# A hybrid decoder trunk on one core: heads cut into steps of one engine each and issued by a running count of the engines' time

## The chip, the cores and the metric

The kernel runs on one core of one Trainium2 chip. The core has TensorE (PE, with its weight loads shown apart as PEld), VectorE (DVE), ScalarE (ACT), GpSimd (POOL) and SyncE (SP, which here only issues DMAs). The metric is the device time of one execution in microseconds, from the hardware; lower is better. The time before is the median of three executions.

## What is computed

Two layers. Each projects x (512 x 2048) with one combined weight matrix, runs three groups of heads (128 columns each), gates every head, projects back, and normalises:

```python
h = x @ w_in                                    # split into fq fk fv fg f_logit  dq dk dv dg  iq ik iw  mq mg
# A) 6 forgetting heads: causal softmax(q k' * scale + c_query - c_key) v, c = cumsum(log_sigmoid(f_logit + b))
# B) 6 sparse heads: rotary q and k; an indexer of 16 small heads picks 128 keys per query; softmax over these
# C) 4 heads into 256 memory tokens: k and v from mem @ w_mem_kv
y = concat(fox, dsa, mem) * silu(gates)
y = y @ w_out
x = layer_norm(alpha * x + y, gain, bias)
```

All of it is float32 accuracy. Every matrix product is made of three matmuls on rounded operands: with a = ah + al and b = bh + bl, it is ah bh + ah bl + al bh. `hi` is made by ACT (a copy that rounds), `lo` by DVE (a subtraction); this pair is called a split.

## The kernel before

**Stages and chunks.** The weights are cut into blocks of 128 x 2048, called chunks, in the order in which TensorE uses them (`stream`). A layer has: the memory's values and keys (`mv`, `mk`), a small block with the indexer's keys and the forget logits (`small`), eight blocks of indexer queries (`iq`), the products for everything that is read by rows (`vs`: the queries and keys of the first four heads of each group, all values, all gates, the memory heads' queries and gates), eight blocks for the queries and keys of the last two heads of each group (`fq 4`, `fk 4`, `fq 5`, `fk 5`, `dq 4`, `dk 4`, `dq 5`, `dk 5`: the head chunks), and the output's products (`out`).

**Fast products.** The `vs` and `out` products use a scheme with seven block products in place of eight (`PRODUCTS`, line 72). Their weight blocks are sums and differences of the stored ones: T1, T3, T2 = T1 + a block, T4 = T2 + a block. Before the change they come about in four ways (`product`, lines 127 to 140): as they are stored (`wall`); summed in DRAM by DMAs on GpSimd's queue and then loaded (`sum`, made by `weight_sums`, line 423); `pair`, two blocks fetched and added on DVE (`pair_w`, line 278: values' T1 for pairs 1 to 5); or `grown`, where a DMA on GpSimd's queue adds a block onto weights that are in SBUF already (`grow_w`, line 286, and `make_w`): in the output, T2 for product Q6 is grown out of P7's T3, and T4 for Q4 out of Q6's. The values run twice over six pairs of columns: a first pass of ten chunks per pair (P1, P7, P2, Q6, Q4), then a second of four (Q5, Q3).

**Loads and splits.** While TensorE works on half-chunk n, the loop (from line 1203) issues the load of a chunk two further on (SP), the growth or pair addition of a later half, and the split of half n + 3 (`split_w`). Seven buffers hold raw weights, four hold splits; 69 slots of 128 x 512 hold everything else, and PSUM has eight banks.

**What sets the order of the heads.** Each engine runs its own queue in order. Work beside the chunks is written as Python generators that are put on a list by `begin` and moved on by `tick`, one step per call. `tick` is called at the middle and at the end of a chunk, and in the head chunks also a quarter of the way in and after three quarters. `TURNS` (line 52) fixes by hand at which half-chunk a head starts (`head_turn`, line 1026). A head (`attend`, line 748) has these steps:

1. scores into three PSUM banks (L224 to L226 through `product`), then on DVE the bias and the row's maximum (L767), on ACT the exponential with its sum (L771). The normalisation (L775 on DVE, L778 on ACT) is put off to the list `before`, which is emptied at a few places in the loop.
2. load of the gates (SP, L999), a turn later load of the values.
3. transposes of the probabilities (L792), their split.
4. transposes of the gates, tanh on ACT and a product on DVE (`gate`, line 507), split of the values (vh on ACT, vl on DVE, L804).
5. the product with the values (L810), and on DVE the gated result (L523).

A step that has operations on several engines issues them all at once, so a PE instruction of the step stands in PE's queue behind what it needs from ACT and DVE in the same step or the step before. Queries and keys of the first four heads of a group are loaded, transposed and split by `qk_head` (line 1013), those of the last two come out of the head chunks (lines 1333 to 1341). `rope` (line 591) does its last addition on GpSimd for loaded heads, on DVE for heads out of chunks. A forgetting head's bias is made on GpSimd (`forget_bias`, line 673). `all_sums` (line 462) issues the DRAM sums a few ticks apart: the values' in the index stage and the values, the output's T3 and T1 in the head stage and the output.

**The output.** Its products read the heads' results as left operands. P1 and P7 need the first eight heads, Q6 and later products all sixteen. `early_operands` and `first_difference` make the first operands during the last head chunks, `late_operands` the rest.

Of the kernel before, what the change touches and what calls it, by code (L numbers as in the profile page):

```python
# [33 lines left out]
SCALE = HD ** -0.5  # L34

# [16 lines left out]
TURNS = {1: ("f", 1), 2: ("d", 0), 3: ("f", 4), 5: ("d", 1), 6: ("f", 2), 7: ("f", 5), 9: ("d", 2),  # L52
         10: ("f", 3), 11: ("d", 4), 13: ("d", 3), 15: ("d", 5)}
MEM_TURNS = {3: 3}
# [39 lines left out]
PAIRED = {"T1": ((0, 0), (0, 1))}  # L94
# [26 lines left out]
def stream():  # L121
# [53 lines left out]

@with_exitstack
def kernel(
# [13 lines left out]
    nc = tc.nc  # L191
# [3 lines left out]
    slots = ctx.enter_context(tc.tile_pool(name="slots", bufs=69))  # L195
# [10 lines left out]

    def slot(name, dt=F32, w=512):
        return slots.tile([P, w], dt, tag="s", name=uid(name))
# [7 lines left out]
    def split(src, hi, lo):  # L216
        nc.scalar.activation(hi, src, AF.Copy)  # L217
        nc.vector.tensor_tensor(lo, src, hi.bitcast(F32), op=ALU.subtract)  # L218
# [30 lines left out]
    def load_w(i, pieces=2, some=(0, 1)):  # L249
        if i < len(chunks) and chunks[i][4][0] != "grown":  # L250
# [3 lines left out]
            if chunks[i][0] == "out" and chunks[i][2][0] == "P7":  # L254
# [86 lines left out]

    held = {i for pair in lends.values() for i in pair}
# [35 lines left out]
    make_identity(nc, ident)  # L378
# [65 lines left out]
    def paced(gen, steps=3):  # L444

        n = 0
        for _ in gen:
            n += 1
            while now[1] == "kv":
                yield 1  # L450
            yield {"heads": 2, "out": 3, "index": 1 + n % 2}.get(now[1], steps)

    def value_sums(l):

        for p in range(PAIRS + 1):
            for n, pair in ((0, p), (1, p - 1)):
                if 0 <= pair < PAIRS:
                    yield from weight_sums("val", l, ("T3",), (pair,), (n,))
        for n in range(2):
            yield from weight_sums("val", l, ("T1",), range(IN_DRAM), (n,))  # L460

    def all_sums():


        for l in range(DEPTH):
            yield from paced(value_sums(l))
            while now != (l, "heads"):
                yield 1
            yield from paced(weight_sums("out", l, ("T3", "T1"), range(2)))
# [10 lines left out]
    before = []  # L480
# [18 lines left out]
    def run_all():  # L499
        while active:  # L500
            tick()

    gates, qs, ks = {}, {}, {}
    ys, left = {}, {}
    masks, chosen, making = {}, set(), []

    def gate(key, ps):

        t = slot("tanh")
        nc.scalar.activation(t, ps, AF.Tanh, scale=0.5)  # L510
        nc.vector.scalar_tensor_tensor(t, t, 1.0, ps, op0=ALU.add, op1=ALU.mult)
        gates[key] = t

    def heads_out(n, key, po):
# [4 lines left out]
        for t in range(2):  # L519
            if e == 0:  # L520
# [3 lines left out]
                                           g[:, c], op0=ALU.mult, op1=ALU.mult)  # L524

# [10 lines left out]
    def mem_head(l, j):  # L536
        load_head(("mq", j), MEMQ, j)
        km = slot("kmem", F32R)
        nc.sync.dma_start(km.bitcast(F32), km_d[l][j])
        yield 3  # L540
        tp = turned(("mq", j), "qk")
        q = slot("qh", F32R), slot("ql", F32R)
        split(tp, *q)
        yield 1
        k2 = (km[:, 0:256], km[:, 256:512])
        ps = [bank("sm"), bank("sm")]
        for qb in range(4):
            product(ps[qb // 2][:, (qb % 2) * 256:(qb % 2 + 1) * 256],
                    tuple(a[:, qb * P:(qb + 1) * P] for a in q), k2, True, True)
        nm, sums, rec = small("nm", 4), small("sums", 4), small("rec", 4)  # L550
        pr = [slot("pm"), slot("pm")]
# [3 lines left out]
        nc.vector.tensor_scalar(nm, nm, SCALE, None, op0=ALU.mult)  # L555
        for qb in range(4):
            cols = slice((qb % 2) * 256, (qb % 2 + 1) * 256)
            nc.scalar.activation(pr[qb // 2][:, cols], ps[qb // 2][:, cols], AF.Exp,
                                 bias=nm[:, qb:qb + 1], scale=SCALE, accum_out=sums[:, qb:qb + 1])
        del km, k2, q  # L560
        vm = slot("vmem", F32R)
        nc.sync.dma_start(vm.bitcast(F32), vm_d[l][j])
        load_head(("mg", j), MEMQ + 1, j)
        yield 1
        nc.vector.reciprocal(rec, sums)
        yield 1
# [939 lines left out]
```

## Time and profile before

| | |
|---|---|
| time, median of 3 runs | 1951.5 us (1949.57 to 1953.13) |
| the profiled execution: time, span | 1955.5 us, 1953.7 us |
| mean granted TensorE clock | 0.993 |
| ACT busy, POOL busy | 1056.9 us (54%), 450.3 us (23%) |
| DMA | 495 MB in 190900 packets, mean 253 GB/s |

The span is from the first to the last instruction of one execution; the time of that execution is 1.8 us more. Busy times of the engines overlap. A row of the table of stretches gives the busy time of each engine in one stretch of the span; a row of the groups gives a line of the kernel, the engine, what is written from what, the shape, how often, its busy time, the mean length of one in nanoseconds, and the idle time of the engine ahead of it with what ended most of it. A matmul's length there includes its way through the array, so matmuls overlap; the distance from one start to the next is what one costs.

### The profile page before, as it was taken

Reading aid. Unit: us, or ns where it says so; the run is one execution under the profiler, and the core shown is the slowest. Engines: PE = TensorE matmul, PEld = TensorE weight load, DVE = VectorE, ACT = ScalarE, POOL = GpSimd, SP = SyncE. Lnnn points to the kernel's source line nnn. Section 1 sums busy time; section 2 is a strip of 40 time slices with the busy share of each in tenths; the row PEclk is TensorE's granted clock in tenths of the full one; section 3 lists DMA queues with packets and bytes.
Section 4 is the critical chain, followed back from the end, with each engine's and each line's share of the span. In section 5 each row is a group of like instructions: output and inputs, shape, how many; then the busy total and the mean of one; then the engine's idle time right before and its main releaser. Section 6 shows DMA issues by size and latency. Waiting matters only on the chain.

```text
span 1953.7 us, 26942 instructions
## 1 busy us (share of the span) xinstructions
PE 1897.2 (97%) x9218; PEld 1604.7 (82%) x9218; DVE 1525.5 (78%) x2455; ACT 1056.9 (54%) x1690; POOL 450.3 (23%) x659
## 2 busy tenths in 40 slices
PE   9999999999999999999999999999999999899997
PEld 8998888888888877787889988888888788777886
DVE  6889778888666667778887897889886666677898
ACT  5776444445455665555476764444454556655553
POOL 0122112211112222271041231211111122222611
PEclk9999999999999999999999999999999999999999
DMA  9888889989999676999878899887799996759975
GB/s 351 297 238 216 248 256 266 279 243 275 324 304 288 210 189 173 283 221 303 283 228 278 243 239 276 264 252 222 210 272 324 310 284 210 189 173 292 260 223 140
DMA packets 190900, 495.17 MB, mean 253 GB/s; under 512 B 18656, under 2 KB 71904, under 8 KB 184172
## 3 DMA queue, kind: packets, MB, share of 16 engines
q1 hardware_dynamic: 144204, 295.24, 44.3%
q0 software_dynamic: 46560, 198.23, 41.6%
q8 instruction: 72, 1.18, 0.2%
q14 instruction: 64, 0.52, 0.1%
HBM read 439.89 MB, written 147.87 MB: 301 GB/s over the span
## 4 chain that ended last, share of the span: by engine, by line
PE 74%; DVE 10%; ACT 6%; DMA 5%; issue 4%; POOL 1%; SPq 0%; DVEq 0%; ACTq 0%; POOLq 0%
PE v L224 16%; PE v L226 16%; PE v L225 16%; PE c L226 4%; PE c L224 4%; PE c L225 4%; PE z L225 3%; PE z L226 3%; PE z L224 3%; DVE wlo L218 2%; DMA raw<-in_wall_dram 2%; DVE rope L595 1%; ACT bt L771 1%; ACT whi L217 1%; DVE pthl L218 1%
## 5 line engine op out<-in xcount | busy, mean ns | idle before, releaser
L218 DVE TENSOR_TENSOR wlo<-raw,whi 128x1024 fp32r<-128x1024 f32 (+1 forms) x497 | 605.2, 1223 | 245.1 <-ACT whi L217 243.1
L217 ACT ACTIVATE whi<-raw 128x1024 fp32r<-128x1024 f32 (+1 forms) x497 | 523.3, 1056 | 458.8 <-PE v L226 308.5
L224 PE MATMUL v<-whi,vxh 128*128 128x512 f32 x768 | 300.3, 391 | 3.2 <-ACT vraw L980 3.2
L226 PE MATMUL v<-whi,vxl 128*128 128x512 f32 x768 | 299.1, 389 | 0.0
L225 PE MATMUL v<-wlo,vxh 128*128 128x512 f32 x768 | 298.9, 389 | 0.0
L224 PE MATMUL v<-whi,xh 128*128 128x512 f32 x576 | 224.2, 389 | 0.0
L226 PE MATMUL v<-whi,xl 128*128 128x512 f32 x576 | 224.1, 389 | 0.0
L225 PE MATMUL v<-wlo,xh 128*128 128x512 f32 x576 | 224.1, 389 | 0.0
L224 PE MATMUL c<-xh,whi 128*128 128x512 f32 (+1 forms) x544 | 202.3, 372 | 0.1
L226 PE MATMUL c<-xh,wlo 128*128 128x512 f32 (+1 forms) x544 | 199.3, 366 | 0.0
L225 PE MATMUL c<-xl,whi 128*128 128x512 f32 (+1 forms) x544 | 198.5, 365 | 0.0
L225 PE MATMUL z<-wlo,yh 128*128 128x512 f32 (+1 forms) x434 | 169.1, 390 | 5.9 <-DVE wlo L218 5.9
L224 PEld LDWEIGHTS v<-whi,vxh 128*128 128x128 f32 x768 | 144.2, 188 | 33.5 <-ACT vraw L980 4.0
L226 PEld LDWEIGHTS v<-whi,vxl 128*128 128x128 f32 x768 | 144.1, 188 | 30.4
L224 PE MATMUL z<-whi,yh 128*128 128x512 f32 (+1 forms) x434 | 168.6, 389 | 0.0
L225 PEld LDWEIGHTS v<-wlo,vxh 128*128 128x128 f32 x768 | 144.2, 188 | 29.4
L226 PE MATMUL z<-whi,yl 128*128 128x512 f32 (+1 forms) x434 | 167.9, 387 | 0.0
L226 PEld LDWEIGHTS v<-whi,xl 128*128 128x128 f32 x576 | 108.1, 188 | 22.6
L224 PEld LDWEIGHTS v<-whi,xh 128*128 128x128 f32 x576 | 108.1, 188 | 22.6
L225 PEld LDWEIGHTS v<-wlo,xh 128*128 128x128 f32 x576 | 108.1, 188 | 22.4
L992 POOL DMA_DIRECT2D v<-vraw x96 | 52.5, 548 | 273.9 <-DVE vraw L969 148.6
L226 PEld LDWEIGHTS c<-xh,wlo 128*128 128x128 f32 x544 | 102.4, 188 | 12.1
(224 smaller groups left out, 3494.4 us busy)
## 6 DMA issues: line engine op xcount, KB each, us to landing
raw<-in_wall_dram SPq DMA_DIRECT2D x330, 512.0 KB, 7.2
sum<-in_wall_dram POOLq DMA_DIRECT2D x44, 1024.0 KB, 11.0
raw<-sum SPq DMA_DIRECT2D x72, 512.0 KB, 8.1
v<-vraw POOLq DMA_DIRECT2D x144, 256.0 KB, 6.7
raw<-in_wall_dram POOLq DMA_DIRECT2D x56, 512.0 KB, 8.0
vraw<-v SPq DMA_DIRECT2D x96, 256.0 KB, 5.2
other<-in_wall_dram SPq DMA_DIRECT2D x80, 256.0 KB, 9.1
grown<-in_wall_dram POOLq DMA_DIRECT2D x64, 256.0 KB, 9.8
```

The source lines that it names most:

```text
L217: nc.scalar.activation(hi, src, AF.Copy)
L218: nc.vector.tensor_tensor(lo, src, hi.bitcast(F32), op=ALU.subtract)
L224: nc.tensor.matmul(ps, ah, bh, start=start, stop=False, skip_group_check=more)
L225: nc.tensor.matmul(ps, ah, bl, start=False, stop=False, skip_group_check=more)
L226: nc.tensor.matmul(ps, al, bh, start=False, stop=stop, skip_group_check=more)
L595: nc.vector.tensor_tensor(t2[a:a + n], ps[b:b + n], sin[b:b + n], op=ALU.mult)
L771: nc.scalar.activation(pr[b][:, off:off + w], pr[b][:, off:off + w], AF.Exp, bias=nm[:, qb:qb + 1], scale=-1.0, accum_out=sums[:, qb:qb + 1])
L992: nc.gpsimd.dma_start(to, t)
```

## The change

Heads are no longer moved on by `tick` at fixed turns. Their generators yield ahead of each piece of work the engine that does it, how many PSUM banks it takes, a time ahead of which it must not be issued, and a condition. `Clock` keeps a running count of each engine's time while the program is written out, with a price by engine, operation and size. `advance`, called after every product of three matmuls in the head, values and output chunks, issues those pieces whose inputs are done by the count, whose banks are free and whose engine is not far ahead of PE. At most three heads are in work at once (`ACTIVE`), and a head waits until enough slots are free (`enough`). Ahead of an output product, `drain` issues head pieces until that product's operands have been issued.

Other edits: the normalisation of the probabilities goes from ACT to DVE; the low half of the values' split and the last addition of every rotary head go to GpSimd; the loads of gates and values come at a head's start. The weight splits of the head chunks are pieces with a due time as well. In the values, T3 for pairs 1 to 5 is fetched as two blocks and added by GpSimd, not summed in DRAM. In the output, T2 is summed in DRAM and loaded, and P7's weights aren't kept. `all_sums` issues at another pace and goes on to the output's sums directly. The first operands of the output are made when the first eight heads are done, the differences when the output begins. The residual's stores come one tick after its scaling. The diff, cut to its core:

```diff
+SOON, LATER, URGENT, DUE = 0.7, 4.0, 5.0, 14.0
+SLOTS = 69
+PACE = 8
+R_ATTEND, R_QK, R_LOAD, R_MEM = 4, 5, 4, 8
+START = (("f", 0), ("f", 1), ("d", 0), ("f", 4), ("d", 1), ("f", 2), ("m", 3), ("f", 5), ("d", 2),
+         ("f", 3), ("d", 4), ("d", 3), ("d", 5))
+ACTIVE = 3
-PAIRED = {"T1": ((0, 0), (0, 1))}
+PAIRED = {"T1": ((0, 0), (0, 1)), "T3": ((0, 1), (1, 1))}
-            if name in GROWN:
+            if name in GROWN and (kind == "val" or name == "Q4"):
...
+class Clock:
+    def charge(self, eng, op, args, kw):
+        if eng == "PE":
+            n = args[0].shape[-1]
+            if op == "transpose":
+                took = 0.109 if n == P else 0.06
+            else:
+                took = max(n / 2400 + 0.0134, 0.058)
+            self.at["PE"] += took
+            return
...
+                took = 0.00105 * n + (0.17 if op == "tensor_tensor_reduce" else 0.07)
...
+                took = 0.003 * n + 0.2 if op == "tensor_tensor" else 0.0008 * n + 0.27
+        self.at[eng] = max(self.at[eng], self.at["PE"], self.floor) + took
...
+    def enough(n):
+        return now[1] == "out" or live() + n <= SLOTS - 2 * KT - 3
...
-                nc.vector.tensor_tensor(d, d, others.pop((i, 2 * h + e)), op=ALU.add)
+                eng = nc.gpsimd if chunks[i][2][0] == "P7" else nc.vector
+                eng.tensor_tensor(d, d, others.pop((i, 2 * h + e)), op=ALU.add)
...
+            yield from paced(weight_sums("out", l, ("T3", "T1", "T2"), range(2)))
+            while l + 1 < DEPTH and now[0] == l:
                 yield 1
-            yield from paced(weight_sums("out", l, ("T3", "T1"), range(2)))
...
+    def fits(f, room):
+        eng, t = f[2], clock.at["PE"]
+        if f[4] is not None and not f[4]():
+            return False
+        if eng == "PE":
+            return f[0] <= t and f[3] <= room
+        return f[0] <= max(t, clock.at[eng]) and clock.at[eng] <= t + (SOON if now[1] == "heads" else LATER)
+    def advance():
+        while flows:
+            t = clock.at["PE"]
+            freed[:] = [x for x in freed if x > t]
+            room = 8 - banks["main"] - banks["held"] - len(freed)
+            some = [f for f in flows if fits(f, room)]
+            if not some:
+                return
+            step_flow(min(some, key=lambda f: f[5] if f[6] > t + URGENT else -1.0))
+    def drain(done):
+        start = clock.at["PE"]
+        while not done():
+            advance()
+            if not done():
+                clock.at["PE"] += 0.2
...
+        def scores(b, blocks):
+            yield "PE", 1
+            ps = bank("s")
...
+            yield "DVE",
...
+            yield "ACT",
...
+        yield "DVE", 0, 0.0, after(scored, 3)
+        nc.vector.reciprocal(rec, sums)
...
+            nc.vector.tensor_scalar(pr[b][:, c], pr[b][:, c], rec[:, qb:qb + 1], None, op0=ALU.mult)
...
+        def values_of():
+            yield "ACT", 0, v_there
...
+            split_hi(t, v[0])
+            yield "POOL",
+            nc.gpsimd.tensor_tensor(v[1], t, v[0].bitcast(F32), op=ALU.subtract)
...
+        yield "PE", 1, 0.0, after(turns, 5)
...
+            drain(lambda: (PRODUCTS[name][1], 2 * col + 1) in left)
...
+            if (kind, j) in HEAD_CHUNKS:
+                splits[n + 3] = flow(split_steps(n + 3), 1e9, clock.at["PE"] + DUE)
+            else:
+                split_w(n + 3)
```

More of the change, by code (lines that the diff above doesn't have):

```diff
@@ L340, in split_w, with split_steps @@
                 raw[i][h] = None
+    def split_steps(n):
+        i, h = divmod(n, 2)
+        if i < len(chunks):
+            r = raw[i][h]
+            hi = whl.tile([P, H], F32R, tag="whi", name=uid("whi"))
+            lo = whl.tile([P, H], F32R, tag="wlo", name=uid("wlo"))
+            qs = [(r, slice(0, H))]
+            if isinstance(r, list):
+                qs = [(r[c], slice(c * 512, (c + 1) * 512)) for c in range(2)]
+            yield "ACT",
+            for t, q in qs:
+                split_hi(t, hi[:, q])
+            yield "DVE",
+            for t, q in qs:
+                split_lo(t, hi[:, q], lo[:, q])
+            parts[n] = (hi, lo)
+            if i not in grows and i not in held:
+                raw[i][h] = None
+    splits = {}
     held = {i for pair in lends.values() for i in pair}
@@ L442, in weight_sums, with paced @@
                         yield
[L444 removed]
+    def paced(gen, steps=PACE):
         n = 0
@@ L448, in paced @@
             n += 1
-            while now[1] == "kv":
+            while now[1] in ("kv", "second"):
                 yield 1
-            yield {"heads": 2, "out": 3, "index": 1 + n % 2}.get(now[1], steps)
+            yield {"heads": 1, "out": 3, "index": 1 + n % 2}.get(now[1], steps)
     def value_sums(l):
[L455 to L460, printed above, removed]
+        for name in ("T3", "T1"):
+            for n in range(2):
+                yield from weight_sums("val", l, (name,), range(IN_DRAM), (n,))
     def all_sums():
@@ L578, in mem_head @@
             hi, lo = slot("pth", F32R), slot("ptl", F32R)
-            split(tp, hi, lo)
+            yield "ACT",
+            split_hi(tp, hi)
+            yield "DVE",
+            split_lo(tp, hi, lo)
+            free(1, "DVE")
             pt.append((hi, lo))
         del pr
-        yield 1
-        gate(("m", j), turned(("mg", j), "gt"))
-        yield 1
+        yield from gate(("m", j), ("mg", j), there)
+        yield "PE", 1
         po = bank("po")
@@ L764, in attend, with after @@
+        def after(done, n):
+            return lambda: len(done) == n and max(done) <= clock.at["PE"]
+        for b, blocks in ((2, (3,)), (0, (0, 2)), (1, (1,))):
+            flow(scores(b, blocks), age)
+        yield "DVE", 0, 0.0, after(scored, 3)
+        del q, k
+        nc.vector.reciprocal(rec, sums)
         for qb in (3, 1, 0, 2):
@@ new lines, in attend, with turn @@
+        pt = {}
+        def turn(tb, kts):
+            yield "PE", 1, clock.at["DVE"] + ahead["DVE"]
+            tp = bank("pt")
+            for kt in kts:
+                _, toff = PT_PACK[kt]
+                for qb in range(kt, 4):
+                    b, off, w = PACK[qb]
+                    nc.tensor.transpose(tp[:, toff + (qb - kt) * P:toff + (qb - kt + 1) * P],
+                                        pr[b][:, off + kt * P:off + (kt + 1) * P], ident)
+            yield "ACT",
+            w = PT_W[tb]
+            both = raws.tile([P, H], F32R, tag="raw", name=uid("pthl")) if w == 512 else slot("pthl", F32R)
+            pt[tb] = both[:, :w], both[:, w:2 * w]
+            split_hi(tp[:, :w], pt[tb][0])
+            yield "DVE",
+            split_lo(tp[:, :w], *pt[tb])
+            free(1, "DVE")
+            turns.append(clock.at["DVE"] + ahead["DVE"])
@@ new lines, in gates_of @@
+        def gates_of():
+            yield from gate(key, ("g", key), there)
+            turns.append(clock.at["DVE"] + ahead["DVE"])
+        def values_of():
+            yield "ACT", 0, v_there
+            v = slot("vh", F32R), slot("vl", F32R)
+            t = vraw.pop(("v", key))
+            split_hi(t, v[0])
+            yield "POOL",
+            nc.gpsimd.tensor_tensor(v[1], t, v[0].bitcast(F32), op=ALU.subtract)
+            rest.append(v)
+            turns.append(clock.at["POOL"] + ahead["POOL"])
@@ L834, in late_operands, with at, operand_steps @@
+        def at(n, i=None):
+            return lambda: (now[1] == "out" and place_out[0] >= n
+                            and (i is None or all(ORDER[8 + 2 * i + e] in heads_done for e in (0, 1))))
+        def operand_steps(name, i, t):
+            yield "ACT",
+            left[name, i] = slot("yh", F32R), slot("yl", F32R)
+            split_hi(t, left[name, i][0])
+            yield "DVE",
+            split_lo(t, *left[name, i])
         for i in range(4):
-            t = ys.pop((0, 1, i))
+            yield "DVE", 0, 0.0, at(2, i)
+            t = ys["S2", i] = ys.pop((0, 1, i))
```

472 lines of the change are left out of this document (294 added, 178 removed).

## The prediction

> **What bounds the kernel now.** I read the page's first part, then the busy time of each engine in stretches cut where the kind of chunk changes, then TensorE's waits, then the groups by shape inside the head stretch and single rows there.
>
> ```profile
> PE 1897.2 (97%) x9218; PEld 1604.7 (82%) x9218; DVE 1525.5 (78%) x2455; ACT 1056.9 (54%) x1690; POOL 450.3 (23%) x659
> ```
>
> TensorE is busy 97% of the span, so whatever the change brings must come out of the rest, or out of busy time that isn't work. The stretches show where that lies (start:end, length, then busy time of PE, PEld, DVE, ACT, POOL, granted clock, DMA share):
>
> ```profile
> 203.70:258.10 54.40, 54.40 (x242) 45.05 (x241) 40.67 (x61) 24.49 (x26) 10.19 (x15) 1.00 0.86 242
> 1343.50:1397.90 54.40, 54.40 (x241) 45.05 (x241) 48.08 (x65) 24.49 (x26) 8.90 (x14) 1.00 0.74 223
> sum 544.00, PE 544.00 PEld 450.45 DVE 452.14 ACT 251.10 POOL 104.36; mean PE 54.40 PEld 45.05 DVE 45.21 ACT 25.11 POOL 10.44
> 542.90:616.80 73.90, 72.54 (x345) 60.14 (x343) 46.80 (x58) 41.59 (x68) 13.23 (x20) 1.00 0.98 306
> 616.80:804.00 187.20, 172.58 (x920) 145.28 (x917) 128.31 (x287) 109.87 (x257) 47.43 (x80) 0.96 0.71 202
> 855.50:971.20 115.70, 111.25 (x481) 89.47 (x481) 90.35 (x140) 55.70 (x77) 26.08 (x35) 1.00 0.97 286
> 1593.90:1779.80 185.90, 169.78 (x920) 141.49 (x918) 128.10 (x287) 109.94 (x257) 47.46 (x80) 0.99 0.71 203
> ```
>
> The first two rows are the values products of pairs 1 (layer 0) and 4 (layer 1); the sum row is over all ten such stretches (pairs 1 to 5, both layers). PE never stops there: 10 chunks of 24 matmuls with 512 columns take 54.40, so one takes 54.40 / 240 = 0.2267 us. The fifth and seventh rows are the head stages (fq 4 up to the first output product). There PE is idle for 14.6 and 16.1 us, and the matmuls that count as busy are stretched too, which its work shows:
>
> ```profile
> L224 PE MATMUL c<-xh,whi 128*128 128x512 f32 x128 | 52.3, 409 | 0.0
> L224 PE MATMUL s<-qh,qh 128*128 128x512 f32 x11 | 6.0, 541 | 3.8 <-ACT qh L217 3.8
> L224 PE MATMUL po<-pthl,vh 128*128 128x512 f32 x10 | 4.4, 438 | 3.3 <-ACT vh L217 3.3
> L1006 PE MATMUL qk<-ident,vraw 128*128 128x128 f32 x64 | 9.5, 274 | 0.0
> L1006 PE MATMUL gt<-ident,vraw 128*128 128x128 f32 x51 | 8.0, 285 | 0.0
> L792 PE MATMUL pt<-ident,bt 128*128 128x128 f32 x60 | 7.6, 273 | 0.0
> L792 PE MATMUL pt<-ident,pr 128*128 128x128 f32 x50 | 6.6, 275 | 1.4 <-ACT pr L778 1.3
> L577 PE MATMUL ptm<-ident,pm 128*128 128x128 f32 x16 | 2.8, 286 | 0.4 <-ACT pm L569 0.2
> ```
>
> ```profile
> 686.88 0.39 PE L224 MATMUL po<-pthl,vh 128*128 128x512 f32 x1
> 688.74 0.63 PE L1006 MATMUL qk<-ident,vraw 128*128 128x128 f32 x4
> 689.12 0.47 PE L224 MATMUL c<-xh,whi 128*128 128x512 f32 x1
> ...
> 790.70 0.80 PE L226 MATMUL po<-pthl,vl 128*128 128x512 f32 x1 [3.40 <-DVE vl L218]
> 793.42 0.73 PE L224 MATMUL s<-qh,qh 128*128 128x512 f32 x1
> ```
>
> An undisturbed head product (12 matmuls, 686.88 to 688.74) takes 1.86 us, and four transposes 0.38. So the stage's work without a stall is 3 x 128 chunk matmuls x 0.2267 = 87.0; 11 scores and 10 value products x 1.86 = 39.1; 241 transposes x 0.095 = 22.9; and for the memory heads about 7 (42 matmuls, 24 of half the columns: 18 x 0.2267 + 24 x 0.113 = 6.8): 155.8 us. The stages take 187.2 and 185.9, so **31.4 and 30.1, together 61.5 us, are not work**. About half is plain waiting. The other half is what follows a wait: after the 3.40 us wait at 790.70 ten matmuls, which go from 687.34 to 688.74 at full speed (1.86 less two of 0.2267 = 1.40), take 2.72. What is waited for:
>
> ```profile
> PE po L226 <- DVE vl L218: 8.7, 6, 3.4
> PE s L224 <- ACT qh L217: 7.6, 6, 2.7
> PE po L224 <- ACT vh L217: 6.3, 6, 1.5
> PE z L225 <- DVE wlo L218: 5.9, 10, 2.4
> PE pt L792 <- ACT pr L778: 2.7, 2, 1.3
> ```
>
> These are pieces of heads that the fixed turns put into PE's queue before ACT and DVE had done them: the split of the values (vh, vl) stands right ahead of the product that reads it, that of the queries (qh) right ahead of the scores. The fourth row is the output's.
>
> **The change part by part.**
>
> *Heads in steps.* No matmul is added or removed. Every PE step of a head enters PE's queue only when the count says that its inputs are done, and chunk matmuls go ahead meanwhile (384 in the stage, then the first four output steps). So all four head waits go, and with them the slow stretches: up to 61.5 us. What is late next is DVE. It is busy for 128.3 of 187.2 us, and gets the normalisation from ACT; prices for this and the next part:
>
> ```profile
> L1072 DVE TENSOR_SCALAR z<-z,mv,rs 128x512 f32<-128x512 f32 x16 | 9.3, 628 | 0.3
> L218 DVE TENSOR_TENSOR vl<-vraw,vh 128x512 fp32r<-128x512 f32 x24 | 17.4, 724 | 0.0
> L596 POOL TENSOR_TENSOR rope<-rope,rope 128x512 f32<-128x512 f32 x16 | 27.9, 1746 | 103.5 <-DVE rope L595 97.5 <-PE po L225 6.0
> L218 DVE TENSOR_TENSOR xl<-xraw,xh 128x512 fp32r<-128x512 f32 x16 | 10.5, 685 | 0.0
> L1094 DVE TENSOR_TENSOR xl<-xf,xh 128x512 fp32r<-128x512 f32 x8 | 10.4, 1306 | 0.1
> L218 DVE TENSOR_TENSOR wlo<-raw,whi 128x1024 fp32r<-128x1024 f32 x493 | 602.4, 1228 | 238.5 <-ACT whi L217 236.5
> ```
>
> A head's 1280 columns of probabilities cost DVE at most 1280 / 512 x 0.628 = 1.57 us, for 11 heads 17.3; off it go ten vl (0.72 each, 7.2) and three rope adds of chunk heads (0.69 each, 2.1): 136.3 us. The 22 vl and rope adds then on GpSimd take 1.75 each, 1.0 more than on DVE: that lengthens a head, and other heads and chunk matmuls cover it. But they also slow DVE. The two xl rows are one operation: 0.685 alone, 1.306 where GpSimd does every second one. So a GpSimd add beside DVE costs DVE 0.62 (the near row, which I take), none if it meets an idle DVE, and its whole 1.75 at worst. That makes 136.3 + 22 x 0.62 = 149.9 us, which fits under 155.8 with little air, and the count knows nothing of the 13.6. I take it that most of these, 10 us a layer, still show as waits of PE (bounds 3, if the queues catch up, and 19, the longest of DVE's sums, 174.8, less 155.8). **Heads: -61.5 + 20 = -41.5 us.**
>
> The rule of the Trainium skill, SBUF — State Buffer, section "Who interferes with whom", is harsher than my price: a VectorE instruction with two SBUF inputs and a GpSimd instruction that reads SBUF exclude each other for a whole instruction. By it an add would cost DVE up to its whole length, and the sum would be that of the slower rival below; the row (0.62) shows that on average part of the block falls where DVE had other work or none.
>
> *Values' T3.* For pairs 1 to 5 the block sums are no longer made in DRAM; each half of a P7 block is fetched with two halves of the other block, and GpSimd adds them: 2 blocks x 2 halves x 2 adds = 8 per pair, 80 in all. Two places can pay. DVE: 452.1 + 80 x 0.62 = 501.7 of 544, still under PE. GpSimd's queue, on which accumulating DMAs and stores now stand behind the adds:
>
> ```profile
> 301.14 6.06 SPq L267 DMA_DIRECT2D raw<-sum  x4
> other<-in_wall_dram SPq DMA_DIRECT2D x80, 256.0 KB, 9.1
> 313.18 1.14 POOL L992 DMA_DIRECT2D v<-vraw  x2 [9.94 <-DVE vraw L976]
> 323.46 0.86 POOL L297 DMA_DIRECT2D raw<-in_wall_dram  x1 [1.85 <-DVE wlo L218]
> 324.06 1.05 ACT L217 ACTIVATE whi<-raw 128x1024 fp32r<-128x1024 f32 x1
> 331.53 0.39 PE L224 MATMUL v<-whi,vxh 128*128 128x512 f32 x1
> ```
>
> For pair 3 of layer 0: the loads of P7's four halves go out from 301.14, the first with its other block lands by 301.1 + 0.9 + 9.1 = 311.1. GpSimd then has 8 adds (14.0), two stores (1.14) and two accumulating issues (1.7) ahead of the last half's split: 327.9. Then ACT (1.05) and DVE (1.23): 330.2, where before ACT began at 324.06. PE wants the half at 331.53. So 1.3 us are left and PE doesn't stop; an add of 1.91 would use them up. Bounds: no loss, or 8 x 1.23 - 1.3 = 8.5 us a pair if every add first waits for a wlo. I take 0.5 for each of ten pairs, since 1.75 is the mean beside a busy DVE: **+5 us**.
>
> *Output's T2 fetched.* P7's weights aren't grown into Q6's, but T2 is summed in DRAM in the index and head stages, when GpSimd has room (47.4 busy of 187.2), and loaded: 16 accumulating issues a layer go from the output's busiest part, 8 longer ones are added earlier. In layer 0 PE is idle for 4.5 us in the output from Q6 on (the last but one of the stretches), by the 5.9 of z waits; I expect **-2** (0 to -4.5). In exchange a drain stands ahead of each output product: if the first eight heads aren't done, PE waits there; that is in the 10 above.
>
> *Second values pass.* Three memory heads in steps; PE's 1.4 us idle in the stretch at 542.9, and I take the same for layer 1: **-2** (0 to -3).
>
> *At nothing:* a head's loads of gates and values move up on SP's queue, ahead of its scores; weight loads behind them can wait for a slot there, but they run two chunks ahead (96 matmuls, 21.8 us), and past that PE would wait for the rest. Differences and first splits of the output's operands move behind the head stage (8 DVE operations a layer x 0.685, 5.5 us), under the 21.8 us of the P1 products, of which they'd cost some 2 if DVE came in late; the residual's stores go one tick later on GpSimd's queue, and nobody waits for them before the output; the sums' pace.
>
> **Sum:** -41.5 + 5 - 2 - 2 = -40.5. The profiled run took 1955.5 (span 1953.7), 4 above the median of 1951.5, and would take 1915; the median becomes **1911**.
>
> **The rivals.**
>
> 1. *DVE bounds the head stage.* If each of the 22 adds takes its whole 1.75 off DVE, DVE needs 136.3 + 38.5 = 174.8 us in a stage of 155.8. Then 12.4 and 11.1 are won, not 41.5: 1951.5 - 23.5 - 4 + 5 = 1929. For it: DVE's 69% now, and 0.9 by the milder price. Against: the xl rows.
> 2. *Slower: GpSimd's adds stop PE in the values products.* The same whole price there: 452.1 + 80 x 1.75 = 592 us in stretches of 544, so PE waits 48; with the head stage as in rival 1: 1951.5 - 23.5 - 4 + 48 = 1972. It decides once an add costs DVE more than (544 - 452.1) / 80 = 1.15, or takes over 1.91 on GpSimd. For it: 48.08 of 54.40 in the fullest pair. Against: the xl rows again, and not all of DVE's work there reads two SBUF tiles (the top-k search, results out of PSUM).
> 3. *The stalls only move.* The steps are held back (three heads at once, free slots, the order of the turns) until the output's first product, and the drain there pays it back: no gain, 1951. For it: the same 32 slots of xT stay taken. Against: at 155.8 + 10 us for some eleven heads and three at once, a head may take 45 us.
>
> **How the numbers follow.** The forecast 0.62, rival 1 0.17, rival 2 0.13, rival 3 0.08. This kernel can be told from no change at about 0.2%, 4 us. Faster is the forecast, rival 1 and a little of rival 3: 0.81; same 0.04; slower 0.15. The forecast's own range: heads -55.5 (3 a layer) to -24, values 0 to +15, the rest 0 to -7: 1889 to 1942. Up to 1950 it takes in rival 1 with stalls in the values and part of rival 3; rival 2 stays outside.
>
> **What would show it.** Head stages of about 166 us in place of 187 and 186, with vl, vh and qh gone from PE's waits; DVE at about nine tenths there; 80 GpSimd adds near 1.75 us beside values stretches of still 54.4 to 55; no z wait for wlo in layer 0. It is wrong if a values stretch grows past 56, if PE waits for wlo after P7's halves, or if the first output product begins with a wait for yh or yl of several us.

## The result and the profile after

The changed kernel takes 1904.7 us (median of four runs, 1903.6 to 1910.3) against 1951.8 (1949.6 to 1953.1): ratio 0.9765, 95% interval 0.9744 to 0.9787, 47 us less. The forecast was 1911, in a range of 1889 to 1950. The profiled execution took 1903.6, its span is 1901.8; the span before was 1953.7. The two profiled runs lie 1.1 below and 3.7 above their medians, so the tables below account for 51.9 us, not 47.

The page's first part of the kernel after:

```profile
PE 1876.5 (99%) x9218; PEld 1596.8 (84%) x9218; DVE 1601.2 (84%) x2519; ACT 1003.7 (53%) x1546; POOL 555.7 (29%) x699
```

The matmuls are as many as before, and DVE and GpSimd are busier, as the moved work has it. Cut where a stage's first product starts, the two traces compare like this (us):

| stage | layer 0 before | after | layer 1 before | after |
|---|---|---|---|---|
| memory's keys and values | 47.8 | 48.2 | 58.6 | 55.0 |
| index and first pass, pair 0 | 150.5 | 150.5 | 150.5 | 150.5 |
| values, first pass, pairs 1 to 5 | 272.0 | 272.3 | 272.0 | 278.1 |
| values, second pass | 141.1 | 141.1 | 141.6 | 140.8 |
| head stage | 187.2 | 161.8 | 185.9 | 161.9 |
| output, P1 and P7 | 51.5 | 52.8 | 51.5 | 52.9 |
| output from Q6 on (layer 1: to the end) | 115.7 | 108.8 | 122.4 | 121.8 |

Heads now spill a little further into P1 and P7, so those two rows belong together: 238.7 to 214.6 and 237.4 to 214.8, which is 46.7 of the 51.9. The output of layer 0 gives 6.9, the edge between the layers 3.6; layer 1's first pass takes 6.1 back.

The same stretches as in the prediction, after (one pair of layer 0 and the slowest kind of layer 1, the sum over all ten pairs, the two head stages, the output of layer 0 from Q6 on):

```profile
204.20:258.80 54.60, 54.60 (x241) 44.93 (x240) 42.87 (x61) 23.92 (x26) 20.30 (x21) 1.00 0.92 281
1202.90:1259.40 56.50, 55.03 (x241) 44.91 (x241) 52.37 (x68) 23.92 (x26) 22.51 (x25) 1.00 0.94 284
sum 550.30, PE 546.69 PEld 449.75 DVE 495.56 ACT 246.28 POOL 209.43; mean PE 54.67 PEld 44.98 DVE 49.56 ACT 24.63 POOL 20.94
617.50:779.30 161.80, 159.44 (x903) 138.06 (x902) 138.04 (x313) 89.07 (x206) 62.47 (x87) 1.00 0.79 215
832.20:941.00 108.80, 108.80 (x482) 90.12 (x481) 90.74 (x135) 56.88 (x78) 11.66 (x14) 1.00 0.73 220
1565.30:1727.20 161.90, 159.53 (x903) 138.10 (x902) 137.98 (x313) 89.10 (x206) 62.33 (x87) 1.00 0.79 217
```

PE's idle time in a head stage went from 14.6 and 16.1 us to 2.4, and the clock there is granted in full. In layer 0 a pair still takes 54.4 to 54.6; in layer 1 it takes up to 56.5, with DVE at 52.4 of it. What TensorE still waits for (engine and tile, what it waits for: total, times, longest; every line of the kernel now stands as L228, the helper that counts):

```profile
PE v L228 <- DVE wlo L228: 4.3, 9, 1.1
PE pt L228 <- DVE pr L228: 2.7, 2, 1.4
PE pt L228 <- DVE bt L228: 2.0, 2, 1.0
PE c L228 <- ACT whi L228: 1.9, 1, 1.9
```

The waits for vl, vh and qh, 22.6 us before, are gone. Of the heads only the normalised probabilities (pr, bt) are waited for, 4.7 us. The first row was 0.7 us before: 3.6 of its 4.3 us stand in layer 1's pairs 1 to 5, at the weights of P7, the sums that GpSimd now adds.

### The profile page after: what moved, and what is told of

Same layout as the page of the kernel before. It is cut to its first block, busy times and chain, and to the rows that moved or that the text cites. A ratio compares the mean times of both kernels' runs of the same rounds, so it can differ in the third digit from the quotient of the medians.

```text
span 1901.8 us, 27038 instructions
## 1 busy us (share of the span) xinstructions
PE 1876.5 (99%) x9218; PEld 1596.8 (84%) x9218; DVE 1601.2 (84%) x2519; ACT 1003.7 (53%) x1546; POOL 555.7 (29%) x699
## 5 line engine op out<-in xcount | busy, mean ns | idle before, releaser
L228 DVE TENSOR_TENSOR wlo<-raw,whi 128x1024 fp32r<-128x1024 f32 (+1 forms) x513 | 671.3, 1317 | 185.6 <-ACT whi L228 181.3
L228 ACT ACTIVATE whi<-raw 128x1024 fp32r<-128x1024 f32 (+1 forms) x513 | 538.8, 1056 | 506.3 <-PE v L228 248.7
L228 PE MATMUL v<-wlo,vxh 128*128 128x512 f32 x768 | 300.0, 391 | 3.6 <-DVE wlo L228 3.6
L228 PE MATMUL v<-whi,vxh 128*128 128x512 f32 x768 | 300.6, 391 | 0.0
L228 PE MATMUL v<-whi,vxl 128*128 128x512 f32 x768 | 299.2, 390 | 0.0
L228 PE MATMUL v<-whi,xh 128*128 128x512 f32 x576 | 224.2, 389 | 0.0
L228 PE MATMUL v<-whi,xl 128*128 128x512 f32 x576 | 224.1, 389 | 0.0
L228 PE MATMUL v<-wlo,xh 128*128 128x512 f32 x576 | 224.1, 389 | 0.0
L228 POOL DMA_DIRECT2D v<-vraw x144 | 94.6, 662 | 419.4 <-ACT vraw L228 230.7
L228 PE MATMUL c<-xh,whi 128*128 128x512 f32 (+1 forms) x544 | 203.7, 374 | 0.0
L228 PE MATMUL c<-xh,wlo 128*128 128x512 f32 (+1 forms) x544 | 198.6, 365 | 0.0
L228 PE MATMUL c<-xl,whi 128*128 128x512 f32 (+1 forms) x544 | 198.1, 364 | 0.0
L228 PEld LDWEIGHTS v<-wlo,vxh 128*128 128x128 f32 x768 | 144.2, 188 | 36.4 <-DVE wlo L228 7.3
L228 PEld LDWEIGHTS v<-whi,vxl 128*128 128x128 f32 x768 | 144.2, 188 | 30.1
L228 PE MATMUL z<-wlo,yh 128*128 128x512 f32 (+1 forms) x434 | 167.9, 387 | 1.2 <-DVE wlo L228 1.2
L228 PEld LDWEIGHTS v<-whi,vxh 128*128 128x128 f32 x768 | 144.3, 188 | 29.5
L228 PE MATMUL z<-whi,yh 128*128 128x512 f32 (+1 forms) x434 | 168.3, 388 | 0.0
L228 PE MATMUL z<-whi,yl 128*128 128x512 f32 (+1 forms) x434 | 167.7, 386 | 0.0
L228 POOL TENSOR_TENSOR raw<-raw,other 128x512 f32<-128x512 f32 x80 | 118.2, 1538 | 67.8 <-DMA other<-in_wall_dram 60.8
L228 PEld LDWEIGHTS v<-whi,xl 128*128 128x128 f32 x576 | 108.1, 188 | 22.6
L228 PEld LDWEIGHTS v<-whi,xh 128*128 128x128 f32 x576 | 108.1, 188 | 22.6
L228 PEld LDWEIGHTS v<-wlo,xh 128*128 128x128 f32 x576 | 108.1, 188 | 22.4
```

Of the source, the lines that this page charges most:

```text
L228: return f(*args, **kw)
```

## The experiments

My theory after this result had four parts. The count gives the heads' gain. T3's adds cost DVE time, which runs out in layer 1. Layer 0's output was held up by accumulating DMAs. The other edits don't matter. Each had a rival. The first part held, the second only beside another cause, and the last two fell.

All edits are against the changed kernel, but for one. "Heads" below is the head stage with P1 and P7, by layer (before 238.7 and 237.4, after 214.6 and 214.8); "pairs" is layer 1's pairs 1 to 5 (272.0 and 278.1).

**The count, left out.**

```diff
-            return f[0] <= t and f[3] <= room
+            return f[3] <= room
...
-            return lambda: len(done) == n and max(done) <= clock.at["PE"]
+            return lambda: len(done) == n
```

> The changed kernel, but a PE piece of a head is issued as soon as the piece ahead of it is in the queues and its banks are free, without regard to the count of when its inputs are done. Theory (the count is what takes the waits off TensorE): most of the 61 us of stalls return, head stages of 175 to 190, time 1930 to 1960. Rival (the cut into pieces of one engine, one step per product, is enough by itself): head stages within 3 us of 162, time 1905 to 1911.

Measured: 1997.3 us, ratio to the kernel before 1.0231 (1.0216 to 1.0247). Heads 247.3 and 247.6; the second values pass, with its memory heads, 156.7 and 153.8 in place of 141. TensorE's longest waits:

```profile
PE pt L228 <- DVE pr L228: 22.0, 12, 3.7
PE pt L228 <- DVE bt L228: 18.3, 12, 4.1
PE ptm L228 <- DVE pm L228: 13.1, 8, 2.3
```

Every head now waits for its probabilities. The same pieces, with the count left out for TensorE's alone (it still paces those of the other engines), are slower than the hand-made turns. So the cut into pieces by itself brings nothing, and the rival falls.

**The count, too low by half, and too high by a fifth** (ACT's, DVE's and GpSimd's prices alone; the one edit is shown, the other has `took * 1.2`):

```diff
-        self.at[eng] = max(self.at[eng], self.at["PE"], self.floor) + took
+        self.at[eng] = max(self.at[eng], self.at["PE"], self.floor) + took / 2
```

> The changed kernel, but the count charges half of its prices for ACT, DVE and GpSimd; PE's stay. Theory (it is the count's agreement with the engines that keeps TensorE from waiting): waits for head pieces come back in part, heads and the two products after them 4 to 15 us longer in each layer, time 1913 to 1935. Rival (any count that puts some products between the pieces is enough, since a piece waits for its turn anyway): within 4 us of 1905.

> The changed kernel, but the count charges 1.2 times its prices for ACT, DVE and GpSimd; PE's stay. Theory (a count that is too high delays pieces but doesn't make TensorE wait for them, as one that is too low does): the waits for normalised probabilities shrink from 4.7 us, some work moves from the head stage into the output, time 1900 to 1912. Rival (the stalls only move: late heads are paid at the drain ahead of the output's first products): waits for yh or yl of several us there, 1915 or above.

Measured at half: 1967.6 us, ratio 1.0082 (1.0065 to 1.0099); heads 238.4 and 238.2, all of the gain lost, more than I had expected. At 1.2: 1964.7 us, ratio 1.0063 (1.0045 to 1.0082); heads 229.0 and 228.7, and the output from Q6 on 122.4 and 137.9. The waits, at half first, then at 1.2:

```profile
PE ptm L228 <- DVE pm L228: 12.9, 12, 1.9
PE pt L228 <- DVE pr L228: 6.9, 2, 3.4
PE s L228 <- ACT qh L228: 6.7, 4, 2.2
PE po L228 <- POOL vl L228: 5.3, 2, 2.7
```

```profile
PE z L228 <- DVE yl L228: 18.1, 12, 4.5
PE pt L228 <- DVE pr L228: 12.8, 2, 6.4
PE z L228 <- ACT yh L228: 6.7, 5, 2.0
```

Too low, and pieces are issued early, so TensorE waits inside the head stage (183.8 and 182.1). Too high, and the head stage itself is shorter (156.6 and 156.4), but only because head pieces are put off: P1 and P7 take 72.4 and 72.3 in place of 52.8 and 52.9. TensorE waits there and later in the output for the operands yh and yl, and once in each head stage 6.4 us for probabilities. Here theory and forecast were wrong and the rival right: a count that is too high costs as much. The third rival of the prediction is real, and the prices as they are avoid it.

**T3 of the values: on DVE, in DRAM, and alone.**

```diff
-                eng = nc.gpsimd if chunks[i][2][0] == "P7" else nc.vector
+                eng = nc.vector
```

> The changed kernel, but the 80 additions for values' T3 are done by DVE. Theory (DVE's time is what the values' first pass runs out of): an add costs DVE 0.685 here against about 0.57 lost beside GpSimd, 8 x 0.115 = 0.9 us more per pair, so the layer-1 stretches stay at 55 to 57 or grow by up to 1 each, time 1905 to 1910. Rival (the queue of GpSimd, with stores and accumulating DMAs behind the adds, is what makes the weights late): the stops vanish and the time falls to 1899.

Measured: 1901.0 us, ratio 0.9738 (0.9723 to 0.9752; the changed kernel's interval overlaps it), span 1899.6. Pairs 276.3, between the two theories: DVE is as full as with GpSimd's adds, yet 1.8 us of the 6.1 are gone. That is little: in the versions that leave the first pass's edits alone (the three of the count, T2 grown, the normalisation on ACT) these pairs take 277.5 to 279.8. So it hints at a share of GpSimd's path beside that of DVE's time, and doesn't show it. The stretch over the five pairs, DVE on top, then the changed kernel:

```profile
1145.90:1422.20 276.30, 273.88 (x1201) 224.74 (x1200) 255.44 (x377) 123.33 (x136) 53.49 (x82) 1.00 0.94 289
```

```profile
1146.40:1424.50 278.10, 274.49 (x1202) 224.64 (x1201) 256.66 (x336) 122.59 (x136) 108.54 (x122) 1.00 0.93 286
```

In DRAM again (`PAIRED` without T3, `value_sums` over all pairs at three steps as before):

```diff
-PAIRED = {"T1": ((0, 0), (0, 1)), "T3": ((0, 1), (1, 1))}
+PAIRED = {"T1": ((0, 0), (0, 1))}
...
-            yield from paced(value_sums(l))
+            yield from paced(value_sums(l), 3)
```

> The changed kernel, but values' T3 of all pairs is summed in DRAM again as before. Theory (the adds on GpSimd cost DVE about 0.57 us each and stop TensorE only in layer 1): the five layer-1 stretches of pairs 1 to 5 go from 278.1 back to 272.0 us, the head stages stay near 162, time about 1899. Rival (the DRAM sums were what loaded GpSimd's queue and the DMA engines in the later stages, so fetching T3 helps there): the stretches are won back but head stages or output lose as much or more, 1905 or above.

The later sums now fall behind, and the output loads part of T2 ahead of its second addition. Measured: 1919.2 us, ratio 0.9840 (0.9824 to 0.9857). Pairs 273.8, won back as the theory says. But the output from Q6 on takes 116.5 and 131.5 in place of 108.8 and 121.8, with one big wait:

```profile
PE z L228 <- DVE wlo L228: 13.7, 4, 7.8
```

That is the rival's side: twenty sums more a layer push seven of the output's own into each output. Fetching T3 costs 4 to 6 us where it stands and makes room for the rest.

The kernel before, with T3 fetched and added by GpSimd and nothing else:

```diff
-PAIRED = {"T1": ((0, 0), (0, 1))}
+PAIRED = {"T1": ((0, 0), (0, 1)), "T3": ((0, 1), (1, 1))}
...
-                nc.vector.tensor_tensor(d, d, others.pop((i, 2 * h + e)), op=ALU.add)
+                eng = nc.gpsimd if chunks[i][2][0] == "P7" else nc.vector
+                eng.tensor_tensor(d, d, others.pop((i, 2 * h + e)), op=ALU.add)
...
-        for p in range(PAIRS + 1):
-            for n, pair in ((0, p), (1, p - 1)):
-                if 0 <= pair < PAIRS:
-                    yield from weight_sums("val", l, ("T3",), (pair,), (n,))
-        for n in range(2):
-            yield from weight_sums("val", l, ("T1",), range(IN_DRAM), (n,))
+        for name in ("T3", "T1"):
+            for n in range(2):
+                yield from weight_sums("val", l, (name,), range(IN_DRAM), (n,))
```

> The kernel before with one part alone: values' T3 of pairs 1 to 5 fetched and added by GpSimd, so that 8 value sums a layer are made in DRAM in place of 28. Theory: head stages stay at 186 and 187, layer 1's first values pass goes from 272 to 276 to 279; the output of layer 0 from Q6 on, which held nine of the next layer's sums, falls from 115.7 to 109 to 112; together 1948 to 1953. Rival (less DMA work relieves the heads too): head stages shorter by over 5 each, time under 1943.

Measured: 1963.4 us, ratio 1.0062 (1.0044 to 1.0080). Heads 236.7 and 238.2: the rival falls. But layer 1's pairs take 287.9, not 276 to 279, and layer 0's output stays at 115.4 (six sums of the next layer still fall there, seven before). Neither theory had either. Layer 1's pairs 1 to 5 as a stretch, and what TensorE waits for in it:

```profile
1175.20:1463.20 288.00, 279.10 (x1202) 227.54 (x1201) 259.69 (x336) 123.15 (x136) 102.02 (x116) 0.98 0.83 249
PE v L225 <- DVE wlo L218: 8.3, 7, 2.9
```

It is idle for 8.9 of the 15.9 us lost. The other 7 are matmuls that take longer: PE is busy 279.1 us at a granted clock of 0.98, where the same work took 272.0 at 1.00 before. Something in the change must spare it most of that, and something must free layer 0's output.

**Why only layer 1, and what spares it.** Layer 1's first pass also scales the residual: 24 DVE operations on twelve tiles, each then stored by a DMA on GpSimd's queue. First the scaling left out (so the residual of layer 1 comes without gain and bias):

```diff
-                scale_row(scaled[2], c)
```

> The changed kernel without the multiplication by gain and addition of bias in the residual's rows (24 two-input DVE operations of 0.69 us in layer 1's first values pass are left out; their loads and stores stay). Theory (in layer 1 DVE's time runs out there): pairs 1 to 5 of layer 1 go from 278.1 to 272 to 273 us, time 1898 to 1900. Rival (GpSimd's chain of adds, stores and accumulating DMAs is too long by itself): they stay at 276 or more.

Measured: 1900.5 us, ratio 0.9743 (0.9728 to 0.9758); pairs 272.9. The stretch:

```profile
1148.40:1421.30 272.90, 272.52 (x1201) 225.06 (x1200) 235.30 (x313) 123.42 (x136) 110.87 (x122) 1.00 0.95 293
```

DVE goes from 256.7 to 235.3 with GpSimd's adds still there (110.9), and the stops are gone, as the theory says. But the stores' waits for the scaling go with it, so this run doesn't tell DVE's time from GpSimd's queue. Next the stores' place alone, with DVE's work as it is:

```diff
                 scale_row(scaled[2], c)
+                nc.gpsimd.dma_start(x1_d[st * P:(st + 1) * P, c * 512:(c + 1) * 512], scaled[2])
...
-            yield 1
-            if scaled:
-                st, c, d = scaled
-                nc.gpsimd.dma_start(x1_d[st * P:(st + 1) * P, c * 512:(c + 1) * 512], d)
-                scaled = d = None
-            yield 2
+            scaled = None
+            yield 3
```

> The changed kernel, but the residual's stores are issued on GpSimd's queue right after their scaling, as before, not one tick later. Theory (in layer 1 the stores stand in that queue waiting for DVE, with the adds of T3 behind them, which is why T3 alone cost 15.9 us there and the whole change 6.1): pairs 1 to 5 of layer 1 go from 278.1 to 284 to 289 us, all else as it is; time 1911 to 1916. Rival (the stores' place is worth nothing, as the prediction had it): no difference, 1903 to 1906.

Measured: 1916.3 us, ratio 0.9816 (0.9799 to 0.9832); pairs 290.6, 12.5 more, even over what I expected. The stores' waits on GpSimd's queue in this pass, with the store at once and then one tick later (total, times, longest):

```profile
POOL x L228 <- DVE z L228: 93.1, 12, 17.2
POOL x L228 <- DVE z L228: 47.1, 9, 12.9
```

What counts is whether adds stand behind a waiting store. GpSimd's queue at the start of pair 1 and of pair 4, with the store at once (start, length, what, and in brackets the idle time ahead with its cause):

```profile
1149.16 0.57 POOL L228 DMA_DIRECT2D x<-z  x1 [11.79 <-DVE z L228]
1149.74 2.66 POOL L228 TENSOR_TENSOR raw<-raw,other 128x512 f32<-128x512 f32 x2
...
1325.15 0.54 POOL L228 DMA_DIRECT2D x<-z  x1 [11.14 <-DVE z L228]
1325.70 2.68 POOL L228 TENSOR_TENSOR raw<-raw,other 128x512 f32<-128x512 f32 x2
```

And in the changed kernel:

```profile
1145.81 1.56 POOL L228 TENSOR_TENSOR raw<-raw,other 128x512 f32<-128x512 f32 x1 [7.71 <-DMA other<-in_wall_dram]
...
1155.43 0.56 POOL L228 DMA_DIRECT2D x<-z  x1
...
1313.57 3.44 POOL L228 TENSOR_TENSOR raw<-raw,other 128x512 f32<-128x512 f32 x2 [6.66 <-DVE wlo L228]
...
1321.47 0.57 POOL L228 DMA_DIRECT2D x<-z  x1 [0.41 <-DVE z L228]
```

A store stands in the queue 11.8 and 11.1 us until DVE has scaled its tile, and the adds behind it stand as well: they begin 4.0 and 4.6 us after the pair's first product (1145.7 and 1321.1). One tick later the adds go first, 0.6 and 0.8 us ahead of that product (1146.4 and 1314.4), and the store behind them hardly waits. Stores with no adds behind them wait as long as ever (up to 12.9). This edit, which the prediction had put at nothing, is worth 12.5 us as soon as GpSimd has adds to do. How the 6.1 us that are left divide between DVE's time and this queue, these runs don't show.

**Layer 0's output: growth, or the next layer's sums.**

```diff
-            if name in GROWN and (kind == "val" or name == "Q4"):
+            if name in GROWN:
...
-            yield from paced(weight_sums("out", l, ("T3", "T1", "T2"), range(2)))
+            yield from paced(weight_sums("out", l, ("T3", "T1"), range(2)))
```

(and the split of P7's weights into two tiles, as before)

> The changed kernel, but the output's T2 is grown in SBUF out of P7's T3 again (16 more accumulating DMAs a layer in the output, 8 sums fewer before). Theory (these DMAs on GpSimd's queue held up the residual's loads in layer 0): the output from Q6 on takes 113 to 116 us in layer 0 in place of 108.8, with waits for wlo, layer 1 as it is; time 1909 to 1912. Rival (the stop went because the heads end in better order): no difference, 1903 to 1906.

Measured: 1902.5 us, ratio 0.9748 (0.9733 to 0.9763), span 1899.6; output from Q6 on 108.8 and 121.8, heads 213.2 and 213.8. My theory falls: with all of the accumulating DMAs back the output doesn't slow down. The hold does it:

```diff
-            while l + 1 < DEPTH and now[0] == l:
-                yield 1
```

> The changed kernel, but the next layer's sums are issued as soon as this layer's are, and no longer held until the next layer begins, so that they fall into layer 0's output as before. Theory (those requests on GpSimd's queue, not the growth of weights, held up the residual's loads in layer 0): the output of layer 0 from Q6 on goes from 108.8 to 111 to 116, with DVE waiting for the loaded residual, and the edge between the layers from 55 to 56 to 59; time 1907 to 1915. Rival: no change, 1903 to 1906.

Measured: 1913.9 us, ratio 0.9810 (0.9788 to 0.9832); layer 0's output from Q6 on 119.7, a little over the range; the edge 53.8 (the expected part of it didn't come), layer 1's pairs 282.6. GpSimd in that output, by groups, without the hold, and then what DVE and TensorE wait for:

```profile
L228 POOL TENSOR_TENSOR seen<-mark,mhalf 128x1 f32<-128x1 f32 x7 | 7.8, 1107 | 85.2 <-DVE mark L228 85.2
L228 POOL DMA_DIRECT2D sum<-in_wall_dram x7 | 4.3, 617 | 0.1
```

```profile
DVE z L228 <- DMA z<-in_x_dram: 16.0, 4, 13.3
PE z L228 <- DVE wlo L228: 8.5, 1, 8.5
```

And the kernel before, in the same stage:

```profile
L412 POOL TENSOR_TENSOR seen<-mark,mhalf 128x1 f32<-128x1 f32 x7 | 5.9, 837 | 69.7 <-DVE mark L411 69.7
L441 POOL DMA_DIRECT2D sum<-in_wall_dram x4 | 3.2, 805 | 0.1
```

Each sum is led by a mark on which GpSimd waits for DVE (`pool_waits`). Seven of them hold GpSimd's queue for 70 to 85 us; the residual's loads are issued behind them, DVE waits for the residual, the weight splits stand behind that on DVE, and TensorE waits 8.5 us for one. The change holds back the next layer's sums, and the output of layer 0 is free. Layer 1 has no next layer, which fits that only layer 0 was slow before.

**The normalisation, back on ACT.**

```diff
-            nc.vector.tensor_scalar(pr[b][:, c], pr[b][:, c], rec[:, qb:qb + 1], None, op0=ALU.mult)
+            nc.scalar.activation(pr[b][:, c], pr[b][:, c], AF.Copy, scale=rec[:, qb:qb + 1])
...
-            yield "PE", 1, clock.at["DVE"] + ahead["DVE"]
+            yield "PE", 1, clock.at["ACT"] + ahead["ACT"]
```

> The changed kernel, but the probabilities of the twelve forgetting and sparse heads are normalised by ACT again, as a piece of its own. Theory (the order of issue brings the gain, and which engine normalises hardly matters): head stages within 2 us of 162, the waits for the normalisation ahead of the transposes are now for ACT, time 1901 to 1908. Rival (moving it to DVE is part of the gain, since ACT's piece delays the splits): head stages longer by 4 or more each, 1912 or above.

Measured: 1911.6 us, ratio 0.9791 (0.9775 to 0.9808), between the two; its interval overlaps the changed kernel's. The head stage alone takes 156.4, since more of the heads falls into P1 and P7 (60.7 and 60.3); together they are 217.1 and 216.7, 2 more each. The waits for pr and bt are gone, and others came:

```profile
PE z L228 <- DVE yl L228: 3.7, 2, 1.9
PE po L228 <- DVE pthl L228: 1.5, 2, 0.7
```

The head takes longer through ACT and ends later. Moving the step to DVE, the fuller engine, is worth 2 us a layer in the heads; more isn't shown.

No run takes the other edits out one by one. What the low half of the values' split on GpSimd, the order in `START` and the early loads bring was not measured.

**The three gains together:** T3 on DVE, T2 grown, the residual's rows spread wider.

```diff
-                eng = nc.gpsimd if chunks[i][2][0] == "P7" else nc.vector
+                eng = nc.vector
...
-            if name in GROWN and (kind == "val" or name == "Q4"):
+            if name in GROWN:
...
-            yield from paced(weight_sums("out", l, ("T3", "T1", "T2"), range(2)))
+            yield from paced(weight_sums("out", l, ("T3", "T1"), range(2)))
...
-            yield 2
+            yield 4
```

> A version to beat both kernels: the changed kernel with T3 added by DVE, T2 grown in SBUF as before (eight sums a layer fewer), and the residual's rows spread over five ticks a tile in place of three. Theory (the three gains are in different stages and add up): layer 1's pairs 1 to 5 at 273 to 275, the rest as in the run with T2 grown, 1895 to 1899. Rival (with T3 on DVE the first pass runs out of DVE's time in layer 1 whatever the residual does): 276 or more there, 1899 to 1902.

Measured: 1899.9 us, ratio 0.9740 (0.9719 to 0.9762), span 1896.5. It beats the kernel before; its interval overlaps the changed kernel's, so by these runs the 4.8 us between the medians stay unproven. Pairs 272.9, with DVE busy for 250.1 of them and TensorE idle for 0.4; heads 213.2 in both layers; the second pass of layer 1 takes 144.4 in place of 140.8, where the residual's rows now end, so 3.6 of 5.2 are given back.

## Why the prediction was right, and where its steps were not

The forecast of 1911 is 6 us above the time, from terms whose errors went both ways.

**The mechanism of the heads was right,** and shown: without the count the gain is gone. The term was -41.5 and measured -46.7, because I left 10 us a layer for waits. Taking off the 31.4 and 30.1 us that I had found not to be work leaves 207.3 for the head stage with P1 and P7, and it now takes 214.6 and 214.8, so 7.4 stay. The surcharge was the mis-sized part: DVE was to need 149.9 us, with 13.6 for GpSimd's adds beside it. In the head stage it is busy for 138.0, but some of its work now stands behind the stage, so P1 and P7 have to be taken with it: over both DVE goes from 173.8 to 186.6 us. Counted in the traces operation by operation, what DVE's operations take there beyond the quickest quarter of their kind is 9.5 us in each layer, and 1.7 before. So about 8 of the 13.6 came (and 2.9 for the normalisation of memory heads, which my sum had left out), and rival 1, which took 38.5, falls with it.

**Values' T3: +5 forecast, +0.3 and +6.1 measured, the right size by another split.** The prices hold: 495.6 less 452.1 over 80 adds is 0.54 us of DVE each (forecast 0.62), and the adds themselves take 1.54 (forecast 1.75):

```profile
L228 POOL TENSOR_TENSOR raw<-raw,other 128x512 f32<-128x512 f32 x80 | 118.2, 1538 | 67.8 <-DMA other<-in_wall_dram 60.8
```

In the chain that I worked out for pair 3 of layer 0, the split of P7's last half began 3.6 us ahead of TensorE's use (327.9 and 331.53); in the trace ACT starts it at 329.29, and the half is due at 332.2, so it is 2.9. But I spread the loss over ten pairs alike. In layer 1 two of the signs that I had named for being wrong came: two stretches of 56.5, past 56, and waits for wlo at P7's weights. By the total the term was right; by its place it was not. I had the fuller DVE of layer 1 in my rows (48.08 of 54.40) and didn't ask what makes it fuller; it is the residual's scaling, and its stores stand in the very queue whose chain I had added up.

**"At nothing" was wrong for the residual's stores.** The step said that nobody waits for them before the output. Nobody waits for the stored tiles, but T3's adds stand behind the stores on GpSimd. The price, if the edit were missing, is 12.5 us. By luck the edit was there, so the sum didn't show the mistake.

**The output: -2 forecast, -6.9 in layer 0, and the cause was wrong.** I put it to fetching T2, but growing T2 again changes nothing there. It is the hold in `all_sums`, which I had listed among the sums' pace at nothing. The trace of before showed the stall in one layer only, and it showed what layer 0's output had on GpSimd's queue and layer 1's had not: seven of the next layer's sums.

**The second pass: -2 forecast, -0.8 measured.** The gain of 3.6 at the edge between the layers I did not see; the versions of the changed kernel take 53.8 to 57.7 us there, with the hold or without, and the kernel before with T3 alone 56.3, in place of 58.6. The same stage of layer 0, 47.8 before, takes 46.0 to 48.7 in them. So part of the gain may be chance, and its cause stays open.

**The rivals.** The second (GpSimd's adds stop TensorE, slower in all) came about in the small: 6 us with the stores moved, 16 in the kernel before with T3 alone, which made that slower by 0.6%. The third, at 0.08, was nearer than that says: a count a fifth too high is enough for it.

## What to carry to other kernels

When an order of issue is made from a count of the engines' time, the prices are the kernel: measure them from the trace, since 20% too high or half too low each cost more than the whole gain here. Before an engine's queue gets compute work, list every DMA issue in it that waits for another engine; each of those waits can become a wait of the new work behind it. And when a stall shows in one layer of two, look for what only that layer's queues hold before taking the nearest cause.

## What the runs showed of the hardware

A GpSimd add holds up a DVE subtraction of two SBUF tiles that meets it. The timeline of the changed kernel, layer 0, pair 3, and the split's group by its least, median and longest duration:

```profile
321.54 2.85 POOL L228 TENSOR_TENSOR raw<-raw,other 128x512 f32<-128x512 f32 x2
321.66 5.09 DVE L228 TENSOR_TENSOR wlo<-raw,whi 128x1024 fp32r<-128x1024 f32 x2
```

```profile
L228 DVE TENSOR_TENSOR wlo<-raw,whi x513: 691/1220/4101, 4.8 to 1877.3; 128x1024 fp32r<-128x1024 f32 x169, 128x512 fp32r<-128x512 f32 x2
```

Two subtractions of 1.22 us take 5.09, that is 2.65 longer, about the 2.85 of two adds in a row; the longest single one takes 4.10, where before it was 2.04. On the average over the 80 adds it is 0.54; more than half of the 513 subtractions take no longer than before (their median is 1.22). The rule of the Trainium skill (SBUF — State Buffer, section "Who interferes with whom": a VectorE instruction with two SBUF inputs and a GpSimd instruction that reads SBUF exclude each other for the whole instruction) agrees with these rows for a single meeting; as a price per add it would have been three times too high here.

An operation with one SBUF tile as its input can be held up as well. In the head stage of layer 0 DVE normalises 256 columns of a forgetting head in 0.873 us on the mean and 512 columns in 0.569, which looks odd until the mean is taken apart. The four operations of one head (512, 256, 128 and 384 columns), first for a head with no GpSimd operation beside it, then for one with two:

```profile
628.84 1.27 DVE L228 TENSOR_SCALAR bt<-bt,rec 128x512 f32<-128x512 f32 x4
...
675.06 1.29 POOL L228 TENSOR_TENSOR rope<-rope,rope 128x512 f32<-128x512 f32 x1
675.81 2.63 DVE L228 TENSOR_SCALAR bt<-bt,rec 128x512 f32<-128x512 f32 x4
676.30 1.47 POOL L228 TENSOR_TENSOR vl<-vraw,vh 128x512 fp32r<-128x512 f32 x1
```

They take 1.27 us and 2.63. Of the twelve operations on 256 columns in both layers, six take 0.35 us with nothing on GpSimd, and six take 1.37 to 1.45; each of these six overlaps a GpSimd subtraction of the values' split (vl) and ends 0.15 us after it. So the move of the normalisation to DVE and the move of vl to GpSimd got in each other's way in half of the forgetting heads.
